# Sleeping set-up threads, a later request for output weights and later parameter transposes in a four-stage transformer kernel

## The chip, the cores and the metric

One core of one Trainium2 chip runs the whole program. The metric is the device time of one execution in microseconds (us). The built program fixes for each engine the order of its instructions; the engines are TensorE (PE; its weight loads are PEld), VectorE (DVE), ScalarE (ACT), GpSimd (POOL) and SyncE (SP, which here issues DMAs).

## The reference

Two blocks work on 512 tokens of width 1024, in float32. The lines that bear on the change, cut down:

```
# layer A: differential attention
q, k = rms_norm(h @ w_q), rms_norm(h @ w_k)          # 8 heads x 2 x 64
lam  = exp(sum(lam_q1*lam_k1)) - exp(sum(lam_q2*lam_k2)) + lam_init
bias = rel_table[t5_bucket(pos_q - pos_k)]           # positions are an input
a    = softmax(where(causal, q @ k.T / 8 + bias, -1e30))
o    = (a[:, 0] - lam * a[:, 1]) @ v                 # then rms_norm per head
h    = h + o @ a_w_o
# conv-gated FFN, twice (l = 0, 1): width-3 causal convolution with ffn_conv_w[l], ffn_conv_b[l]
h    = h + (silu(g) * a) @ ffn_w_out[l];  h = h + (p[l] @ w_proj) * sigmoid(rms_norm(h) @ w_gate)
# layer B: latent attention; its low-rank projection w_dkv is 1024 x 320
# second block: sparse attention (bias rows from rel_bias), convolution, gated linear
# attention, then a gated FFN, a per-layer embedding and a last norm
```

## The kernel before, in words

**Arithmetic.** A float32 matrix product is made of three products in the format fp32r: each operand is split in a high and a low part, and `mm3` issues low weight x high data, high weight x high data, high weight x low data. A weight arrives by DMA in a raw buffer `wr` (two buffers, issued by SP); ACT writes its high part `wh`, DVE the low part `wl = gain*wr - wh`. The data's parts are the tiles `X_83` (high, written by ACT from a transposed PSUM tile) and `X_84` (low, DVE). In attention the same split gives `qs`, `kh` (ACT) and `qs`, `kl` (DVE), each from a PSUM tile `tr` of four transposed 128x128 blocks.

**PSUM.** Accumulators have four banks, transposes two (`tr`), and two more (`s`) serve scores and transposes. A bank is written again only when its last reader is done, so a `tr` group on the PE waits for the DVE and ACT copies of the group two before it.

**Order of the work.** The program is written as generator threads (class `Order`): a thread gives way by yielding a planned time, a flag or a free bank, and the loop resumes whichever is due by a planned clock. `sleep(ns)` yields a planned time that many nanoseconds ahead, `due()` the planned end of what is recorded, `wait(flags)` until others have set them, `bank("tr")` until a bank is planned free. A tile scheduler then puts every engine's instructions in their final order. Nearly all instructions carry the line of a helper: L148 (recording), L285 (`mm`), L295 (`tr`). DMAs of weights are L378, of parameter rows `colr` L360.

**Start of layer A** (`layer_a`, from L711). The four token tiles are normed (`xn = h*ss`), transposed and split into `X`. Around that stand the test whether positions are consecutive (`pos_test`: tiles `praw`, `p`, `fl`, `posfi`; its result is loaded by every engine at L607, and L610 branches over a block that ordinary positions don't need), minus lambda (tiles `lt`, `ls`, `nlam`; four broadcasts issued on POOL at L733) and the bias rows (`rel_rows`: one-hot `oh` times table `tb`, result `rv`, stored as `rowsA`). These are recorded in line, not in threads.

**Middle of layer A.** `produce` makes four pairs of heads' queries and keys and two halves of values in the order p0 v0 p1 p2 p3 v1, then the product with `a_w_o`, whose four first weight tiles are 128x1024. `fqk[3]` are the flags of the last pair's four token tiles. `lane` runs the attention of the pairs: `sb = s + xn` (bias), exponentials `wT`, then `o`, normed to `on` by `sub_norm`.

**Parameters** (`columns`, L649). Its last part, `third` (L683), transposes `ffn_conv_w`, `ffn_conv_b` of l = 0 and l = 1 (tiles `cw0`, `cw1`) and the second block's convolution parameters from raw rows `colr` to columns, one PE transpose and one DVE copy each.

**Start of layer B** (L1127). The four token tiles t0 to t3 are multiplied with the 320 columns of `w_dkv`: 24 matmuls each. Beside it stand the rope tables (`ang`, `rn`, `rr`, `sin`, `cos`, with gains `kr`, `qr`), the norms of what comes out (`cn`, `kx`, `ky`, `kz`) and the second block's bias rows (`rel_rows` again, stored as `rowsR`), recorded in line ahead of the tiles.

Of the kernel before, what the change touches and what calls it, by code (L numbers as in the profile page):

```python
# [184 lines left out]
class Model:  # L185
    def __init__(self, ctx, tc, I, O):
        self.tc, self.I, self.O = tc, I, O
        self.n, self.rings = 0, {"acc": [], "tr": [], "s": []}
        self.od, self.g = Order(), {}
        nc = self.nc = Issue(self.od, tc.nc)  # L190
        self.acc, self.wu, self.xs, self.cr, self.sl = Slots(4), Slots(WB), Slots(2), Slots(3), Slots(2)
        pool = lambda name, **k: ctx.enter_context(tc.tile_pool(name=name, **k))
        self.cp = pool("cp", bufs=1)
        self.hp = pool("hp", bufs=1)
        self.wp = pool("wp", bufs=4)
        self.st = pool("st", bufs=4)
# [152 lines left out]
    def rows_T(self, out, rows):  # L349
# [17 lines left out]
        self.cr.give()  # L367


    def weight(self, n, parts, gain=None):  # L370
# [165 lines left out]

    def rel_rows(self, pp, table, name):

        nc = self.nc
        tb = pp.tile([33, 8], F32, name=self.uid("tb"), tag="tb")  # L540
        nc.vector.memset(tb, NEG)
        nc.scalar.dma_start(tb[:32, :], table)
        oh = pp.tile([33, 640], F32, name=self.uid("oh"), tag="oh")
        nc.scalar.dma_start(oh, self.I["c_onehot"])
        rv = pp.tile([8, 640], F32, name=self.uid("rv"), tag="rv")
        for c0, n in ((0, 512), (512, 128)):
            ps = self.ptile("tr")
            self.mm(ps[:8, :n], tb, oh[:, c0:c0 + n], True, True)
            nc.vector.tensor_copy(rv[:, c0:c0 + n], ps[:8, :n])
        row = self.dp.tile([8, 640], F32, name=name, tag=name)  # L550
        nc.sync.dma_start(row, rv)
        return row

# [24 lines left out]

    def pos_test(self, la):

        nc = self.nc
        fi = la.tile([1, 1], I32, name="posfi", tag="posfi")
        with self.phase("pos0") as pp:
            T = lambda shape, dt, tag: pp.tile(shape, dt, name=self.uid(tag), tag=tag)
            raw = T([1, S], I32, "praw")
            nc.scalar.dma_start(raw, self.I["positions"])
            hf, lf = self.pos_parts(T, raw, [1, S])
            dh, dl = T([1, S - 1], F32, "p3"), T([1, S - 1], F32, "p4")
            nc.vector.tensor_sub(dh, hf[:, 1:], hf[:, :S - 1])
            nc.vector.tensor_sub(dl, lf[:, 1:], lf[:, :S - 1])  # L590
            nc.vector.scalar_tensor_tensor(dl, dh, 4096.0, dl, op0=ALU.mult, op1=ALU.add)
            nc.vector.tensor_scalar(dl, dl, 1.0, None, op0=ALU.not_equal)
            fl = T([1, 1], F32, "fl")
            nc.vector.tensor_reduce(fl, dl, axis=AX.X, op=ALU.max)
            nc.vector.tensor_copy(fi, fl)
        return fi

# [51 lines left out]
    def columns(self, first):  # L649
# [33 lines left out]
        def third():  # L683
# [4 lines left out]
            self.cw = []  # L688
            for l in range(2):
                w = cp.tile([P, 176], F32, name=f"cw{l}", tag=f"cw{l}")  # L690
                self.cw.append(w.rearrange("p (i m) -> p i m", i=4))
# [19 lines left out]
    def layer_a(self, nxt):  # L711
# [11 lines left out]
        with self.phase("la") as pp:  # L723
            T1 = lambda name: pp.tile([P, 1], F32, name=name, tag=name)

            B = [self.rel_tile(f"biasB{i}", [1 + NT, 2]) for i in range(4)]
            fi = self.pos_test(pp)
            self.columns(False)
            qg, kg, sg = self.g["a_q_norm"], self.g["a_k_norm"], self.g["a_sub_norm"]

            lt = pp.tile([P, 4, 64], F32, name="lt", tag="wT", bufs=WTS)
            for i, nm in enumerate(("a_lam_q1", "a_lam_k1", "a_lam_q2", "a_lam_k2")):
                nc.gpsimd.dma_start(lt[:, i, :], I[nm][0].partition_broadcast(P))  # L733
            ls = pp.tile([P, 2], F32, name="ls", tag="ls")
            nc.vector.tensor_mul(lt[:, 0, :], lt[:, 0, :], lt[:, 1, :])
            nc.vector.tensor_mul(lt[:, 2, :], lt[:, 2, :], lt[:, 3, :])
            nc.vector.tensor_reduce(ls[:, 0:1], lt[:, 0, :], axis=AX.X, op=ALU.add)
            nc.vector.tensor_reduce(ls[:, 1:2], lt[:, 2, :], axis=AX.X, op=ALU.add)
            nc.scalar.activation(ls, ls, AF.Exp)
            nlam = T1("nlam")  # L740
            nc.vector.tensor_sub(nlam, ls[:, 1:2], ls[:, 0:1])
            nc.vector.tensor_scalar(nlam, nlam, -LAM_INIT, None, op0=ALU.add)

            flags = lambda: [Flag() for _ in range(NT)]
# [59 lines left out]
            def produce():  # L804
                for job in A_ORDER.split():
                    yield from (pair if job[0] == "p" else values)(int(job[1]))
                made.done = True

                for c in range(2):
# [13 lines left out]
            def fetch():  # L823
                for i, t in [(i, t) for i in range(4) for t in range(NT)]:
                    n = (t + 1) * P
                    if t == 0 and i < 3:
                        self.rel_fill(B[i + 1][0], row[2 * i + 2:2 * i + 4])
                    yield from self.xs.take()
# [11 lines left out]
            def lane():  # L840
                while steps:
# [16 lines left out]
                    if ob[1] == 4:  # L858
                        od.add(self.sub_norm(pp, ob[0], t, half, sg, made, fo[half][t], qns, obs), 0)

            od.add(produce(), 1)
            with self.phase("rel") as pr:
                row = self.rel_rows(pr, I["rel_bias_table"], "rowsA")
                self.rel_fill(B[0][0], row[:2])
                od.run(begun)
                which.append(self.bias_a(B, fi))
            fB.done = True
# [67 lines left out]
    def ffn_ple(self, x, token_of, src, combine, W_out, gain, p, w_gate, w_proj, ple_gain, nxt, name):  # L935
# [4 lines left out]
        with self.phase(name) as pp:  # L940
# [186 lines left out]
    def layer_b(self, x, nxt):  # L1127
# [3 lines left out]
        with self.phase("lb") as pp:  # L1131
# [11 lines left out]
            with self.phase("lb0") as p0:  # L1143
                cos, sin = self.rope_tables(p0)
                row = self.rel_rows(p0, I["rel_bias_2"], "rowsR")
                gpe = self.bcast_row(p0, I["k_pe_norm"], 64, "gkpe")
# [57 lines left out]
                od.add(down(), 1)  # L1204
                od.run(ready)

                for f in fkv:
# [3 lines left out]
            with self.phase("lb1") as p1:  # L1211
# [4 lines left out]
                def produce():  # L1216
                    for ch in range(8):
# [4 lines left out]
                        if ch == 4:  # L1222
                            self.rel_fill(self.rows_c, row)
                        chunk[ch] = [None, None]
# [760 lines left out]
```

## Time and profile before

| | |
|---|---|
| median of 3 runs | 2270.88 us (2266.21 to 2273.49) |
| profiled execution | 2270.06 us, of which 2268.3 us from the first to the last instruction (the span) |
| PE busy | 2197.4 us, 97% of the span |
| DVE / ACT / POOL busy | 59% / 47% / 8% |
| mean granted PE clock | 0.988 of full speed |

All times of rows are microseconds from the start of the span. Some 71 us of the span have no matmul in them; where these lie and what ended each is read from the timeline of the PE, where a row's bracket gives the idle time before it and the instruction that ended it.

### The profile page before, as it was taken

The page shows a single profiled execution, that of the slowest core. Times are in us where ns is not written, and L with a number is a line of the kernel's source. Part 1 is how long each engine was busy: PE and PEld are TensorE (multiplying, and loading weights), DVE is VectorE, ACT ScalarE, POOL GpSimd, SP SyncE. Part 2 cuts the span into 40 slices and gives each one's busy share as a digit, 9 for nine tenths or more (in the row PEclk, how much of TensorE's full clock was granted, in tenths as well). Part 3 has the DMA queues.
Part 4 walks back from the last instruction along what each step waited for, and adds up shares of the span by engine and source line. Part 5 has one row for each costly group of instructions (what it writes and reads, how often), then busy time and mean ns, then how long its engine had stood idle before and what let it go on. Part 6 is the DMA issues. An engine that isn't in the chain of part 4 may idle for free.

```text
span 2268.3 us, 30282 instructions
## 1 busy us (share of the span) xinstructions
PE 2197.4 (97%) x11166; PEld 1861.9 (82%) x11166; DVE 1336.6 (59%) x2885; ACT 1062.0 (47%) x2102; POOL 173.0 (8%) x232
## 2 busy tenths in 40 slices
PE   7987999999999999999999999999999999999998
PEld 5866798888887888888988888889978888888886
DVE  6668656446545777767565366357977643333344
ACT  4547445334444565555454254254657543323333
POOL 3123000000001121210000000001010000000000
PEclk9999999999999999999999999999989999999999
DMA  6323123332332412212133233234430123323322
GB/s 190 99 63 93 59 84 98 103 98 84 107 98 80 128 43 59 68 40 82 54 107 102 94 103 97 79 98 122 99 91 22 54 66 101 99 91 99 99 89 82
DMA packets 168839, 200.01 MB, mean 88 GB/s; under 512 B 19201, under 2 KB 123709, under 8 KB 168688
## 3 DMA queue, kind: packets, MB, share of 16 engines
q1 hardware_dynamic: 165172, 194.77, 28.1%
q10 hardware_dynamic: 2940, 2.02, 0.3%
q0 software_dynamic: 576, 1.26, 0.3%
q8 instruction: 88, 1.44, 0.3%
q14 instruction: 63, 0.52, 0.1%
HBM read 195.87 MB, written 7.38 MB: 90 GB/s over the span
## 4 chain that ended last, share of the span: by engine, by line
PE 91%; DVE 4%; ACT 1%; DMA 1%; issue 1%; POOL 0%; DVEq 0%; POOLq 0%; SPq 0%; ACTq 0%
PE acc L285 82%; PE s L285 4%; PE tr L295 4%; PE tr L285 1%; DVE wl L148 1%; DVE sb L148 1%; PE s L295 0%; DVE ss L148 0%; DVE X L148 0%; ACT wh L148 0%; DMA xn<-biasB 0%; DVE qs L148 0%; ACT wT L148 0%; DVE qn L148 0%; DMA tb<-rel_bias 0%
## 5 line engine op out<-in xcount | busy, mean ns | idle before, releaser
L285 PE MATMUL acc<-X,wh 128*128 128x512 f32 (+1 forms) x2592 | 734.9, 370 | 4.0 <-DVE X L148 4.0
L285 PEld LDWEIGHTS acc<-X,wh 128*128 128x128 f32 x2592 | 469.9, 189 | 85.0 <-DVE X L148 4.7
L285 PE MATMUL acc<-wh,X 128*128 128x512 f32 (+4 forms) x1664 | 502.0, 380 | 0.2 <-DVE X L148 0.2
L285 PE MATMUL acc<-X,wl 128*128 128x512 f32 (+1 forms) x1296 | 474.7, 369 | 0.0
L148 ACT ACTIVATE wh<-wr,gcol 128x512 fp32r<-128x512 f32 (+5 forms) x480 | 289.6, 656 | 208.4 <-PE acc L285 123.8
L148 DVE SCALAR_TENSOR_TENSOR wl<-wr,gcol,wh 128x512 fp32r<-128x512 f32 (+5 forms) x480 | 306.1, 674 | 131.5 <-ACT wh L148 129.5
L285 PEld LDWEIGHTS acc<-wh,X 128*128 128x128 f32 x1664 | 309.9, 190 | 45.9 <-DVE X L148 0.7
L285 PE MATMUL acc<-wl,X 128*128 128x512 f32 (+4 forms) x832 | 322.4, 388 | 7.3 <-DVE qn L148 3.3
L285 PEld LDWEIGHTS acc<-X,wl 128*128 128x128 f32 x1296 | 244.2, 189 | 40.8
L148 DVE TENSOR_TENSOR wl<-wr,wh 128x1024 fp32r<-128x1024 f32 (+1 forms) x134 | 152.5, 1144 | 183.8 <-ACT wh L148 183.6
L148 POOL TENSOR_TENSOR ss<-ss,mhalf 128x1 f32<-128x1 f32 (+3 forms) x140 | 128.9, 923 | 1727.4 <-DVE ss L148 1703.0
L148 ACT ACTIVATE wh<-wr 128x1024 fp32r<-128x1024 f32 (+1 forms) x134 | 132.5, 995 | 238.9 <-PE acc L285 191.2
L285 PE MATMUL acc<-wh,hh 128*128 128x512 f32 x528 | 205.7, 390 | 0.0
L285 PE MATMUL acc<-wl,hh 128*128 128x512 f32 x528 | 204.5, 389 | 0.0
L285 PE MATMUL acc<-wh,hl 128*128 128x512 f32 x528 | 203.7, 390 | 0.0
L285 PEld LDWEIGHTS acc<-wl,X 128*128 128x128 f32 x832 | 158.1, 190 | 32.8 <-DVE qn L148 3.6
L148 DVE SCALAR_TENSOR_TENSOR cv<-acc,cw,cv 128x511 f32<-128x511 f32 (+1 forms) x176 | 126.1, 745 | 95.2 <-ACT cv L148 94.4
L148 DVE TENSOR_TENSOR h<-h,acc 128x512 f32<-128x512 f32 x120 | 81.6, 684 | 61.3 <-PE acc L285 60.8
L285 PEld LDWEIGHTS acc<-wl,hh 128*128 128x128 f32 x528 | 99.1, 188 | 20.5
L285 PEld LDWEIGHTS acc<-wh,hl 128*128 128x128 f32 x528 | 99.1, 188 | 20.4
L285 PEld LDWEIGHTS acc<-wh,hh 128*128 128x128 f32 x528 | 99.1, 188 | 20.4
L148 ACT ACTIVATE wT<-tr 128x128 f32<-128x128 f32 (+3 forms) x160 | 68.8, 435 | 91.4 <-PE tr L295 90.6
(312 smaller groups left out, 2688.5 us busy)
## 6 DMA issues: line engine op xcount, KB each, us to landing
wr<-ffn_w_in SPq DMA_DIRECT2D x160, 256.0 KB
wr<-ffn_w_out SPq DMA_DIRECT2D x40, 512.0 KB
wr<-ple_w_gate SPq DMA_DIRECT2D x24, 512.0 KB
wr<-ffn_w_gate SPq DMA_DIRECT2D x40, 256.0 KB
wr<-ffn_w_up SPq DMA_DIRECT2D x40, 256.0 KB
wr<-ffn_w_down SPq DMA_DIRECT2D x20, 512.0 KB
wr<-a_w_qkv SPq DMA_DIRECT2D x32, 256.0 KB
wr<-b_w_o SPq DMA_DIRECT2D x16, 512.0 KB
```

What stands on the lines that cost most here:

```text
L148: return fn(*args, **kw)
L285: self.nc.tensor.matmul(out, lhsT=a, rhs=b, start=start, stop=stop)
L295: self.nc.tensor.transpose(out, src, self.ident[:src.shape[0], :src.shape[0]])
```

## The change

1. At the start of layer A the positions' test, minus lambda and the bias rows become three threads (`pos_test`, `minus_lambda`, `rel`, each wrapped by the new `flagged`), started after `produce`. Each issues its DMAs, sleeps 8000, 12000 or 4000 planned ns and then does its work; `pos_test` also yields `due()` between its steps. Lambda's four broadcasts move from POOL's queue to ACT's. The program runs until the three flags are set before it goes on to `bias_a` with the branch.
2. `produce` waits for `fqk[3]` before it asks for the first weights of `a_w_o`.
3. `third` waits for the flag `fed` before the convolution parameters of l = 1; `fed` is set when the first FFN starts. So two transposes and copies of `cw1` and one of the second block's parameters move from layer A to that FFN; their DMAs keep their place on SP to within some rows.
4. In layer B `rel_rows` is a thread with a sleep of 4000 ns, and the wait for its flag stands after the first tiles' flag `ready`.

```
+    @staticmethod
+    def flagged(thread, flag):
+        yield from thread
+        flag.done = True
...
-    def rel_rows(self, pp, table, name):
+    def rel_rows(self, pp, table, name, out):
...
+        yield self.sleep(4000)
         for c0, n in ((0, 512), (512, 128)):
+            yield from self.bank("tr")
...
+    def pos_test(self, pp, fi):
+        raw = T([1, S], I32, "praw")
+        nc.scalar.dma_start(raw, self.I["positions"])
+        yield self.sleep(8000)
...
             for l in range(2):
+                if l:
+                    yield from self.wait(self.fed)
...
                 made.done = True
+                yield from self.wait(*fqk[3])
...
+            def minus_lambda():
+                lt = pp.tile([P, 4, 64], F32, name="lt", tag="wT", bufs=WTS)
+                for i, nm in enumerate(("a_lam_q1", "a_lam_k1", "a_lam_q2", "a_lam_k2")):
+                    nc.scalar.dma_start(lt[:, i, :], I[nm][0].partition_broadcast(P))
+                ls = pp.tile([P, 2], F32, name="ls", tag="ls")
+                yield self.sleep(12000)
...
             od.add(produce(), 1)
...
+                for f, thread in zip(early, (rel(), self.pos_test(pr, fi), minus_lambda())):
+                    od.add(self.flagged(thread, f), 0)
                 od.run(begun)
+                for f in early:
+                    od.run(f)
                 which.append(self.bias_a(B, fi))
...
             od.add(main(), 1)
+            self.fed.done = True
...
-                row = self.rel_rows(p0, I["rel_bias_2"], "rowsR")
+                row, frow = [], Flag()
+                od.add(self.flagged(self.rel_rows(p0, I["rel_bias_2"], "rowsR", row), frow), 0)
...
                 od.run(ready)
+                od.run(frow)
```

**Place 1, the start.** DVE of before, from the second tile's statistic on; `wl_104` is the second weight pair, `lt` the second product of lambda vectors (it needs the third and fourth broadcast):

```order
L148 TENSOR_SCALAR ss_120<-ss_120 128x1
L148 TENSOR_SCALAR p_186<-p_186 1x511
L148 SCALAR_TENSOR_TENSOR wl_104<-wr_102,gcol_86,wh_103 128x512
L148 TENSOR_REDUCE fl_191<-p_186 1x1
L148 SCALAR_TENSOR_TENSOR wl_104<-wr_102,gcol_86,wh_103 128x512
L148 TENSOR_SCALAR xn_119<-h,ss_120 128x1024
L148 TENSOR_TENSOR lt<-lt 128x64
L148 CAST posfi<-fl_191 1x1
L148 TENSOR_TENSOR X_84<-tr_125,X_83 128x4x128
L148 TENSOR_TENSOR X_84<-s_132,X_83 128x4x128
L148 TENSOR_REDUCE ls<-lt 128x1
```

DVE of the change, from the first normed tile `xn_113` (in before it stands behind the two `wl_94`) to the low halves of the first tile's `X_84`:

```order
L148 TENSOR_SCALAR xn_113<-h,ss_114 128x1024
L148 TENSOR_TENSOR p_272<-p_268 1x511
L148 TENSOR_TENSOR praw_273<-p_269 1x511
L148 SCALAR_TENSOR_TENSOR wl_94<-wr_92,gcol_86,wh_93 128x512
L148 TENSOR_TENSOR lt<-lt 128x64
L148 SCALAR_TENSOR_TENSOR wl_94<-wr_92,gcol_86,wh_93 128x512
L148 SCALAR_TENSOR_TENSOR praw_273<-p_272,praw_273 1x511
L148 TENSOR_SCALAR ss_120<-ss_120 128x1
L148 TENSOR_REDUCE ls<-lt 128x1
L148 TENSOR_TENSOR lt<-lt 128x64
L148 TENSOR_TENSOR X_84<-tr_125,X_83 128x4x128
L148 TENSOR_TENSOR X_84<-s_132,X_83 128x4x128
```

ACT of the change, from the first tile's square on:

```order
L148 ACTIVATE xn_113,ss_114<-h 128x1024
L863 DMA lt<-a_lam_q 128x64
L863 DMA lt<-a_lam_k 128x64
L863 DMA lt<-a_lam_q 128x64
L148 ACTIVATE wh_93<-wr_92,gcol_86 128x512 x2
L863 DMA lt<-a_lam_k 128x64
L148 ACTIVATE xn_119,ss_120<-h 128x1024
```

The second `lt` now stands ahead of the first tile's `X_84`, and its fourth broadcast is issued by ACT behind two halves of `wh_93`; the three others are issued ahead of those. DVE's load of `posfi` for the branch (L610, now L618) stands seven rows after the second half of `wl_104`, and half of the next weight's split, `wl_323`, has moved ahead of it.

**Place 2, the middle of layer A.** DVE of before; `tr_3783` and `tr_3810` are the last two groups of transposes of the last pair, `wl_4332` and `wl_4338` the third and fourth weight tile of `a_w_o` (the first two, `wl_3959` and `wl_3965`, stand six and two rows further up):

```order
L148 TENSOR_TENSOR wl_4332<-wr_4330,wh_4331 128x1024
L148 SCALAR_TENSOR_TENSOR qs_3423<-tr_3783,gcol_196,qs_3423 64x2x128
L148 TENSOR_REDUCE ss_4000<-on_3998 128x4
L148 TENSOR_SCALAR ss_4000<-ss_4000 128x4
L148 TENSOR_TENSOR wl_4338<-wr_4336,wh_4337 128x1024
L148 SCALAR_TENSOR_TENSOR qs_3423<-tr_3810,gcol_196,qs_3423 64x2x128
L148 TENSOR_REDUCE ss_4014<-on_4012 128x4
L148 TENSOR_TENSOR on_3998<-o_2556,ss_4000 128x512
L148 SCALAR_TENSOR_TENSOR kl_3425<-tr_3783,gcol_196,kh_3424 64x2x128
L148 SCALAR_TENSOR_TENSOR kl_3425<-tr_3810,gcol_196,kh_3424 64x2x128
L148 TENSOR_SCALAR ss_4014<-ss_4014 128x4
L148 SCALAR_TENSOR_TENSOR qs_3423<-tr_3783,gcol_196,qs_3423 64x2x128
```

DVE of the change, the same stretch; the last two groups are `tr_3747` and `tr_3774`, the weight tiles `wl_4318` and `wl_4324` (the first two stand ten and seven rows further up):

```order
L148 TENSOR_TENSOR wl_4318<-wr_4316,wh_4317 128x1024
L148 SCALAR_TENSOR_TENSOR kl_3410<-tr_3747,gcol_174,kh_3409 64x2x128
L148 TENSOR_TENSOR on_3965<-o_2552,ss_3967 128x512
L148 TENSOR_TENSOR wl_4324<-wr_4322,wh_4323 128x1024
L148 SCALAR_TENSOR_TENSOR qs_3408<-tr_3774,gcol_174,qs_3408 64x2x128
L148 TENSOR_REDUCE ss_3981<-on_3979 128x4
L148 SCALAR_TENSOR_TENSOR qs_3408<-tr_3747,gcol_174,qs_3408 64x2x128
L148 SCALAR_TENSOR_TENSOR kl_3410<-tr_3774,gcol_174,kh_3409 64x2x128
L148 TENSOR_SCALAR ss_3981<-ss_3981 128x4
L148 SCALAR_TENSOR_TENSOR kl_3410<-tr_3747,gcol_174,kh_3409 64x2x128
L148 SCALAR_TENSOR_TENSOR qs_3408<-tr_3774,gcol_174,qs_3408 64x2x128
L148 TENSOR_TENSOR on_3979<-o_2624,ss_3981 128x512
```

All four weight splits still stand ahead of the last keys' `kl`. From the first split to the last `kl` there are 22 rows in before and 27 in the change, where four rows of the first scores' `sb`, which stood behind that `kl`, now stand ahead of it.

**Place 3, the start of layer B.** PE of before, from the last matmuls of t0 and t1 on; `tr_7988` and `tr_7991` are the bias rows, `tr_8143` the high half of tile t2's transposes, `acc_8180` tile t2:

```order
L285 MATMUL acc_8100<-wh_8050,X_83 128x320
L285 MATMUL acc_8100<-wh_8050,X_84 128x320
L285 MATMUL tr_7988<-oh_7985,tb_7982 8x512
L285 MATMUL tr_7991<-oh_7985,tb_7982 8x128
L295 MATMUL tr_8143<-ident,xn_7900 128x128 x4
L285 MATMUL acc_8180<-wl_8027,X_83 128x320
```

PE of the change, from the eighteenth matmul on of those 24 of tile t2 (`acc_8162`); `tr_8084` and `tr_8166` are the bias rows, `tr_8148` and `s_8155` tile t3's transposes, `acc_8219` tile t3:

```order
L285 MATMUL acc_8162<-wl_8039,X_83 128x320
L285 MATMUL acc_8162<-wh_8038,X_83 128x320
L285 MATMUL acc_8162<-wh_8038,X_84 128x320
L285 MATMUL tr_8084<-oh_8010,tb_8007 8x512
L285 MATMUL acc_8162<-wl_8039,X_83 128x320
L285 MATMUL acc_8162<-wh_8038,X_83 128x320
L285 MATMUL acc_8162<-wh_8038,X_84 128x320
L295 MATMUL tr_8148<-ident,xn_8001 128x128 x4
L295 MATMUL s_8155<-ident,xn_8001 128x128 x4
L285 MATMUL tr_8166<-oh_8010,tb_8007 8x128
L285 MATMUL acc_8219<-wl_8015,X_83 128x320
L285 MATMUL acc_8219<-wh_8014,X_83 128x320
```

DVE of the change, from tile t3's norm `xn_8001` on:

```order
L148 TENSOR_SCALAR xn_8001<-h,ss_8002 128x1024
L148 TENSOR_SCALAR ss_8201<-ss_8201 128x1
L148 TENSOR_SCALAR qr_7991<-qr_7991 128x4x32
L148 SCALAR_TENSOR_TENSOR cn_8094<-acc_8045,ss_8087,gckv_7997 128x256
L148 TENSOR_SCALAR kx_8096<-acc_8045,ss_8087 128x64
L148 TENSOR_TENSOR kr_7980<-cos_7972,gkpe_7978 128x4x32 x2
L148 TENSOR_TENSOR qr_7990<-cos_7972,gqpe_7987 128x4x32 x2
L148 SCALAR_TENSOR_TENSOR cn_8137<-acc_8105,ss_8130,gckv_7997 128x256
L148 TENSOR_SCALAR kx_8139<-acc_8105,ss_8130 128x64
L148 TENSOR_SCALAR ss_8201<-ss_8201 128x2
L148 TENSOR_TENSOR ky_8097<-kx_8096,kr_7981 128x32 x2
L148 TENSOR_TENSOR kz_8098<-kx_8096,kr_7980 128x64
```

The bias rows have moved behind t2's matmuls on the PE. On DVE the norm of t3 has moved behind the sine gains `kr`, `qr`; the low half `X_84` of t3 follows one row after this piece.

## Rows read from the trace of the kernel before

**Rows 1.** Page, section 1: busy time, share of the span, instructions.

```profile
PE 2197.4 (97%) x11166; PEld 1861.9 (82%) x11166; DVE 1336.6 (59%) x2885; ACT 1062.0 (47%) x2102; POOL 173.0 (8%) x232
```

**Rows 2.** Timeline of DVE, start: start us, us, what, [idle before <- what ended it].

```profile
9.84 0.23 DVE L148 TENSOR_TENSOR lt<-lt 128x64 f32<-128x64 f32 x1 [2.86 <-DMA lt<-a_lam_k]
...
9.98 1.27 DVE L148 TENSOR_TENSOR p<-p 1x511 f32<-1x511 f32 x2
...
13.23 0.73 DVE L148 TENSOR_SCALAR xn<-h,ss 128x1024 f32<-128x1024 f32 x1
```

**Rows 3.** Timeline of ACT, start.

```profile
0.81 0.53 ACTq L586 DMA_DIRECT2D praw<-positions  x1
...
9.67 1.33 ACT L148 ACTIVATE wh<-wr,gcol 128x512 fp32r<-128x512 f32 x2 [3.87 <-DMA wr<-a_w_qkv]
```

**Rows 4.** Instructions of tile praw: duration ns min/median/max, first and last start us.

```profile
L572 DVE TENSOR_SCALAR p<-praw x1: 414/414/414, 2.3 to 2.3; 1x512 int32<-1x512 int32 x1
```

**Rows 5.** DMAs of tile lt, issued on POOL.

```profile
DMA to landing us min/median/max: 6.1/7.6/7.9
```

**Rows 6.** Timeline of the PE, start.

```profile
14.02 1.12 PE L295 MATMUL tr<-ident,xn 128*128 128x128 f32 x4 [8.80 <-DVE ss L148]
```

**Rows 7.** Timeline of DVE, middle of layer A.

```profile
201.62 1.21 DVE L148 TENSOR_TENSOR wl<-wr,wh 128x1024 fp32r<-128x1024 f32 x1
...
207.82 1.23 DVE L148 TENSOR_TENSOR wl<-wr,wh 128x1024 fp32r<-128x1024 f32 x1 [1.37 <-ACT wh L148]
...
216.76 0.90 DVE L148 SCALAR_TENSOR_TENSOR kl<-tr,gcol,kh 64x256 fp32r<-64x256 f32 x2
...
217.88 0.69 DVE L148 CUSTOM_DVE_ANT_0 sb<-s,xn 128x512 f32<-128x512 f32 x1 [0.23 <-PE tr L295]
```

**Rows 8.** Timeline of the PE, middle of layer A.

```profile
217.40 0.85 PE L295 MATMUL tr<-ident,sb 128*128 128x128 f32 x2 [8.48 <-DVE kl L148]
```

**Rows 9.** Windows: length, busy us (instructions) PE, PEld, DVE, ACT, POOL; granted clock; DMA share.

```profile
120.00:200.00 80.00, 68.02 (x336) 54.70 (x335) 59.44 (x170) 48.47 (x118) 24.30 (x28) 0.96 0.28 81
215.00:220.00 5.00, 2.60 (x9) 2.16 (x10) 4.32 (x11) 3.09 (x9) 2.27 (x3) 0.50 0.02 6
220.00:225.00 5.00, 4.70 (x28) 4.03 (x27) 4.74 (x18) 3.67 (x13) 0.00 (x0) 0.81 0.02 1
738.00:744.00 6.00, 5.31 (x20) 5.01 (x20) 5.67 (x25) 2.81 (x5) 0.00 (x0) 0.50 0.64 201
744.00:747.00 3.00, 2.69 (x19) 2.19 (x17) 1.29 (x7) 1.92 (x7) 0.00 (x0) 0.98 1.00 265
```

**Rows 10.** Instructions of tile colr on the PE: ns min/median/max.

```profile
L295 PE MATMUL tr<-ident,colr x8: 219/241/280, 5.0 to 136.4; 88*128 88x88 f32 x4, 16*128 16x16 f32 x1, 3*128 3x3 f32 x1, 66*128 66x66 f32 x1
```

**Rows 11.** Copies into tile cw on DVE: ns min/median/max.

```profile
L148 DVE COPY cw<-tr x4: 236/246/250, 112.9 to 129.8; 128x88 f32<-128x88 f32 x4
```

**Rows 12.** Timeline of the PE, start of layer B.

```profile
735.31 1.23 PE L285 MATMUL tr<-oh,tb 33*8 33x512 f32 x4 [2.90 <-DMA tb<-rel_bias]
737.09 0.98 PE L295 MATMUL tr<-ident,xn 128*128 128x128 f32 x4 [0.55 <-DVE rv L148]
738.76 0.63 PE L285 MATMUL acc<-wl,X 128*128 128x320 f32 x1 [0.69 <-ACT X L148]
...
746.30 0.41 PE L285 MATMUL acc<-wl,X 128*128 128x320 f32 x1 [0.17 <-ACT X L148]
...
750.36 0.27 PE L295 MATMUL tr<-ident,ky 128*128 128x128 f32 x1
```

**Rows 13.** Timeline of ACT, issue of the table's DMA in layer B.

```profile
730.85 0.33 ACTq L542 DMA_DIRECT2D tb<-rel_bias  x1
```

**Rows 14.** Timeline of DVE, start of layer B, tile t3's norm and after.

```profile
739.81 0.75 DVE L148 TENSOR_SCALAR xn<-h,ss 128x1024 f32<-128x1024 f32 x1
740.47 0.48 DVE L148 TENSOR_TENSOR kr<-sin,gkpe 128x128 f32<-128x128 f32 x2
...
743.66 0.49 DVE L148 TENSOR_TENSOR ky<-kx,kr 128x32 f32<-128x32 f32 x4
```

More of the change, by code (lines that the diff above doesn't have):

```diff
@@ L188, in __init__ @@
         self.n, self.rings = 0, {"acc": [], "tr": [], "s": []}
-        self.od, self.g = Order(), {}
+        self.od, self.g, self.fed = Order(), {}, Flag()
         nc = self.nc = Issue(self.od, tc.nc)
@@ L551, in rel_rows @@
         nc.sync.dma_start(row, rv)
-        return row
+        out.append(row)
     def rel_fill(self, m, row):
@@ L577, in pos_parts @@
         return hf, lf
-    def pos_test(self, la):
+    def pos_test(self, pp, fi):
         nc = self.nc
[L582 to L596, printed above, removed]
+        T = lambda shape, dt, tag: pp.tile(shape, dt, name=self.uid(tag), tag=tag)
+        raw = T([1, S], I32, "praw")
+        nc.scalar.dma_start(raw, self.I["positions"])
+        yield self.sleep(8000)
+        hf, lf = self.pos_parts(T, raw, [1, S])
+        dh, dl = T([1, S - 1], F32, "p0"), T([1, S - 1], F32, "praw")
+        yield self.due()
+        nc.vector.tensor_sub(dh, hf[:, 1:], hf[:, :S - 1])
+        nc.vector.tensor_sub(dl, lf[:, 1:], lf[:, :S - 1])
+        yield self.due()
+        nc.vector.scalar_tensor_tensor(dl, dh, 4096.0, dl, op0=ALU.mult, op1=ALU.add)
+        nc.vector.tensor_scalar(dl, dl, 1.0, None, op0=ALU.not_equal)
+        yield self.due()
+        fl = T([1, 1], F32, "fl")
+        nc.vector.tensor_reduce(fl, dl, axis=AX.X, op=ALU.max)
+        nc.vector.tensor_copy(fi, fl)
     def bias_a(self, B, fi):
@@ L726, in layer_a @@
             B = [self.rel_tile(f"biasB{i}", [1 + NT, 2]) for i in range(4)]
-            fi = self.pos_test(pp)
+            fi = pp.tile([1, 1], I32, name="posfi", tag="posfi")
             self.columns(False)
             qg, kg, sg = self.g["a_q_norm"], self.g["a_k_norm"], self.g["a_sub_norm"]
[L731 to L742, printed above, removed]
             flags = lambda: [Flag() for _ in range(NT)]
@@ L826, in fetch @@
                     if t == 0 and i < 3:
-                        self.rel_fill(B[i + 1][0], row[2 * i + 2:2 * i + 4])
+                        self.rel_fill(B[i + 1][0], row[0][2 * i + 2:2 * i + 4])
                     yield from self.xs.take()
@@ L859, in lane, with rel @@
                         od.add(self.sub_norm(pp, ob[0], t, half, sg, made, fo[half][t], qns, obs), 0)
+            nlam = T1("nlam")
+            def minus_lambda():
[4 more added lines that the diff above has]
+                yield self.sleep(12000)
+                nc.vector.tensor_mul(lt[:, 0, :], lt[:, 0, :], lt[:, 1, :])
+                nc.vector.tensor_mul(lt[:, 2, :], lt[:, 2, :], lt[:, 3, :])
+                nc.vector.tensor_reduce(ls[:, 0:1], lt[:, 0, :], axis=AX.X, op=ALU.add)
+                nc.vector.tensor_reduce(ls[:, 1:2], lt[:, 2, :], axis=AX.X, op=ALU.add)
+                nc.scalar.activation(ls, ls, AF.Exp)
+                nc.vector.tensor_sub(nlam, ls[:, 1:2], ls[:, 0:1])
+                nc.vector.tensor_scalar(nlam, nlam, -LAM_INIT, None, op0=ALU.add)
             od.add(produce(), 1)
             with self.phase("rel") as pr:
-                row = self.rel_rows(pr, I["rel_bias_table"], "rowsA")
-                self.rel_fill(B[0][0], row[:2])
+                row, early = [], [Flag() for _ in range(3)]
+                def rel():
+                    yield from self.rel_rows(pr, I["rel_bias_table"], "rowsA", row)
+                    self.rel_fill(B[0][0], row[0][:2])
+                for f, thread in zip(early, (rel(), self.pos_test(pr, fi), minus_lambda())):
+                    od.add(self.flagged(thread, f), 0)
                 od.run(begun)
+                for f in early:
+                    od.run(f)
                 which.append(self.bias_a(B, fi))
@@ L1222, in produce @@
                         if ch == 4:
-                            self.rel_fill(self.rows_c, row)
+                            self.rel_fill(self.rows_c, row[0])
                         chunk[ch] = [None, None]
```

## The prediction, made before the changed kernel ran

> **What bounds the kernel now.** I read the page first: the PE is busy 2197.4 us [rows 1], so of the span of 2268.3 us only some 71 us hold no matmul. This change adds and removes no product of the GEMMs, so all it can give back lies in those gaps and in stretches that run at the lower clock. I then went through the timeline of the PE for gaps, and for each looked at the engine named in its bracket. Three lie beside edited code. At the start the PE waits 8.80 us for the first normed tile [rows 6]. In the middle of layer A it waits 8.48 us, because the `tr` bank that it wants next is held until DVE has made the last keys' `kl` [rows 8]: from 217.40 - 8.48 = 208.9 on; afterwards the granted clock is 0.50 for five microseconds and 0.81 for five more [rows 9]. At the start of layer B it waits 2.90 us for the bias table's DMA, then 0.55 and 0.69 us [rows 12], and from 738 to 744 the clock is at 0.50, the lower level of 1.2 GHz [rows 9]. A gap counts for the end here, since after each of these the PE goes on with little idle time up to the last stage; what is saved on DVE or ACT alone counts for nothing.
>
> **Edit 1, the start.** What it adds on the issuing side is cheap. The one-hot and table DMAs now precede `praw` on ACT, but ACT has nothing else at 0.81 [rows 3]. Three of lambda's broadcasts go out before ACT's first high parts of weights at 9.67, for which it has stood idle 3.87 us [rows 3]: hidden. If that cover were gone each would cost about the 0.53 us of an issue [rows 3].
>
> What it moves is on DVE. Before, DVE is idle 2.86 us up to 9.84, when lambda's first product finds its data [rows 2]. In the change the first `xn` (0.73 us) and the two position differences (1.27 us) stand ahead of that point, as the order shows; together 2.00 us of work [rows 2] that fills idle time. Against that, the first weight split comes next and has to wait for ACT's first half, 9.67 + 1.33/2 = 10.3 [rows 3], so the chain restarts 0.5 us later than at 9.84. Net 2.0 - 0.5 = 1.5 us less. The PE has its first tile transposed long before 14.02 [rows 6], but without the split it can't multiply.
>
> What it adds is a wait. The second `lt` now stands ahead of the first tile's `X_84`, and its last broadcast is issued by ACT behind both halves of `wh_93`, at 9.67 + 1.33 = 11.0 [rows 3]. DVE gets there at about 12.8: from 10.3, what it did before between 9.84 and 13.23 less the two differences, 3.4 - 1.3 = 2.1 us [rows 2], and some 0.3 us for a statistic and a second reduction (estimates between the rows' 0.23 and 0.73). With a landing time L the wait is L - 1.8 us if positive, and behind it stand `X_84`, the next splits and `xn`, all of which the PE needs, and on ACT the exponential of `ls`. Before holds no broadcast on ACT's queue, so L is bounded by neighbours: `praw`, one row, was issued at 0.81 and used at 2.3, 1.5 us [rows 3, 4]; the table in layer B, on the same queue, was issued at 730.85 and used at 735.31, 4.5 us [rows 12, 13]; the same four broadcasts from POOL landed in 6.1 to 7.9 us [rows 5]. I take 3 us, halfway between the two rows of ACT's queue. The term is -1.5 + 1.2 = **-0.3 us**; the bounds are -1.5 (L at or under 1.8) and -1.5 + 6.1 = +4.6 (L = 7.9).
>
> The Trainium skill, "DMA: Bandwidth & Descriptors", section "Anatomy of one DMA — SWDGE (gpsimd) path", gives about 2.0 us fixed per DMA; no row here lands lambda's broadcasts that quickly, and by that figure this term would be an estimated -1.3 and the whole sum 1 us lower.
>
> **Edit 3, the parameters.** Three PE transposes of 219 to 280 ns [rows 10] and three copies of about 0.25 us [rows 11] leave layer A and are paid again in the first FFN. From 120 to 200 the PE is busy 68.0 of 80 us [rows 9]: it waits there now and then, mostly for DVE, so leaving may save something; in the FFN the transposes are paid in full and the copies hide, since DVE is busy 59% of the span [rows 1]. Gain at most 0.75 (all of DVE's), loss at most 0.75 (all of the PE's, if layer A hid them): **-0.4 us**, because DVE is what is waited for where they stood.
>
> **Edit 2, the wait of `a_w_o`.** If it took the four 128x1024 splits out of DVE's way, the 8.48 us would go, and with it the low clock: 2.60 x 0.5 + 4.70 x 0.19 = 2.2 us [rows 9], 10.7 in all. The built order speaks against that. All four splits still stand among the last pair's `qs` and `kl`, ahead of the last `kl`. So the stall stays, and I compare its length. From the first split, at 201.62, to the end of the last `kl`, 216.76 + 0.90 = 217.66, the 22 rows of before took 16.0 us, 1.37 of them waiting for a weight's high part [rows 7]. In the change there are 27 rows. Four are the first two scores' pieces, 2 x 0.69 = 1.4 us that before paid after the stall [rows 7]; the fifth is one more small statistic or `qs`, about 0.5. With all waits kept, the last `kl` comes 1.9 us later for 1.4 us of work done early, a loss of 0.5; without the 1.37 us of waiting, since the first two weight tiles stand three to four rows further ahead of the others, a gain of 0.9. On the PE the wait is then cut in three, one for each of the last banks, instead of one; its sum stays near 8.5. I take **-1.0 us**, nearer the gain; bounds -10.7 and, with the three waits keeping the clock down for another five microseconds at 0.50, +0.5 + 2.5 = +3.
>
> **Edit 4, layer B.** Of the present wait 2.90 + 0.55 + 0.69 = 4.1 us [rows 12] goes, since t2's matmuls now precede the bias rows. Those 24 take (750.36 - 746.30)/24 = 0.17 us each at nearly full clock [rows 12], 4.1 us in all. The gap before 735.31 began at 732.4; with 0.4 for four transposes moved ahead, t2 is done at about 736.9, and the table has landed by then. What is late next is tile t3: its norm ends at 739.81 + 0.75 = 740.56 now [rows 14]. In the change the rope chain runs while before it waited for the bias row (some 1.9 us earlier), but the norm stands behind the sine gains (0.96 [rows 14] and two small rows, 1.4); `X_84` and one copy leave, 0.96. So 740.56 - 1.9 + 1.4 - 0.96 = 739.1, and the PE waits 2.2 us. Then t3's low half stands behind eleven rows like those from 740.47 to 744.15, 3.7 us [rows 14] less the sine gains' 0.96 plus 0.5 for `kz` and statistics: 739.1 + 3.2 + 0.7 = 743.0, while the PE has transposes and two matmuls up to 740.6, so it waits another 2.4 us. From 743.0 the remaining 22 matmuls take 3.7 us at full clock, end 746.7, against 750.36: -3.7. At the lower clock, which the rows show from 738 to 744 behind the waits of before [rows 9], they take about twice that: end 750.4, no gain. The clock had returned by 744 in before, so part of the stretch is fast: **-2.0 us**, about halfway; bounds -3.7 and 0.
>
> **The rest.** The order of layer A between 25 and 330 is dealt anew by moved times. I put nothing on that and plus or minus 3 us in the range, a quarter of the 12 us in which the PE is idle from 120 to 200 [rows 9].
>
> Sum: -0.3 - 0.4 - 1.0 - 2.0 = -3.7 us. The profiled execution took 2270.06 us (span 2268.3 and 1.8 around it), 0.8 us under the median of 2270.88, so it is typical: 2266.4 on its scale, **2267.2 us** on that of the median.
>
> **The rivals.**
> *A, the middle stall goes.* If the two first splits, further ahead, free DVE in time, the stall and the low clock shrink by most of 10.7 us: 2270.9 - 0.3 - 0.4 - 10.7 - 2.0 = 2257.5. For it: DVE idles 1.37 us there for weights [rows 7]. Against it: the order. Half of it gives 2263.
> *B, a stall of the ring at another place.* Where a weight split lands ahead of the last reader of a `tr` bank, the PE stops as it does at 208.9. One more such place in layer A costs 8.48 + 2.2 us: 2267.2 + 10.7 = 2277.9, slower than before. It decides from a wait of about 4 us on (3.7 to be made up). For it: the whole layer is reordered and its transposes have two banks; against it: DVE's order shows no new pile of splits.
> *C, the fourth broadcast is late.* DVE and ACT then stand at the second `lt`: with POOL's 7.9 us [rows 5] the start term is +4.6 and the sum +1.2, 2272.1; it turns the gain to a loss from L = 6.7. Here the Trainium skill bears on the case: in "DMA: Bandwidth & Descriptors", section "Issuing engines are not separate DMA queues", it says that DMAs of all issuing engines run on the same sixteen engines, so the move would save issue time only; the rows of ACT's queue at 1.5 and 4.5 us lean against POOL's landing times [rows 3, 4, 12, 13].
> *D, layer B gives nothing,* because t3 waits behind rope work at the lower clock: 2269.2.
>
> **How the numbers follow.** The measurement can tell about 0.3%, 6.8 us, from no change, so faster means under 2264.1 and slower over 2277.7. The forecast with its own 2262 to 2271 has 0.48, A whole or half 0.22, B 0.13, C 0.10, D 0.07. Faster: A's 0.22, and a third of the forecast's (start at its lower bound, layer B at -3.7, a good reshuffle: -1.5 - 0.4 - 1.0 - 3.7 - 1 = -7.6), 0.38 in all. Slower: B and a tail of C, 0.14. Same: 0.48. The range runs from A, 2257, to the edge of B, 2277.
>
> **What would show it.** Right: DVE's second `lt` idle by about 1 us on a DMA from ACT; the PE in the middle still short of 8 to 10 us, ended by `kl`, with the four splits before it; in layer B no wait on the table but two of about 2 us, on `xn` and `X`. Wrong: the middle without a wait over 3 us; a wait over 4 us at the start on lambda; a new wait over 4 us on a `tr` reader between 30 and 330 us.

## The result, and the profile after

The changed kernel takes 2282.39 us (median of 5, 2279.13 to 2286.32) against 2270.88 us: ratio 1.0054 with a 95% interval of 1.0036 to 1.0073, some 12 us slower, and outside the range that was forecast. The page of its profiled execution (2280.97 us), section 1:

```profile
PE 2207.1 (97%) x11166; PEld 1869.3 (82%) x11166; DVE 1336.7 (59%) x2885; ACT 1060.8 (47%) x2102; POOL 168.3 (7%) x228
```

The idle time of the PE has hardly changed: 2279.3 - 2207.1 = 72.2 us, against 2268.3 - 2197.4 = 70.9 [rows 1]. It is the busy time that grew, by 9.7 us, and the mean granted clock fell from 0.988 to 0.985, which over the span is 7 us. So most of the loss is work that ran at the low level of the clock, and in layer A above all. The windows from 20 to 330 us, before and then changed (columns as in [rows 9]; the clock is the third number from the end):

```profile
20.00:330.00 310.00, 281.83 (x1495) 235.16 (x1494) 213.30 (x529) 162.74 (x357) 61.24 (x68) 0.96 0.30 89
```

```profile
20.00:330.00 310.00, 275.71 (x1394) 227.48 (x1393) 204.35 (x511) 155.14 (x345) 61.19 (x67) 0.94 0.29 87
```

The timeline of the PE in the changed kernel, its waits beside the edited code and its longest ones in layer A (those of 1.0 to 2.2 us between 20 and 170, of which before has more, are left out):

```profile
14.56 0.80 PE L285 MATMUL acc<-wh,X 128*128 128x512 f32 x1 [2.74 <-DVE X L148]
...
180.26 0.44 PE L295 MATMUL tr<-ident,sb 128*128 128x128 f32 x2 [2.99 <-ACT wT L148]
...
181.87 0.80 PE L285 MATMUL acc<-wl,X 128*128 128x512 f32 x1 [1.17 <-DVE qn L148]
...
214.45 0.63 PE L295 MATMUL tr<-ident,qn 128*128 128x128 f32 x4 [1.59 <-DVE kl L148]
...
221.55 0.45 PE L295 MATMUL tr<-ident,sb 128*128 128x128 f32 x1 [6.48 <-DVE kl L148]
...
222.79 0.47 PE L295 MATMUL tr<-ident,sb 128*128 128x128 f32 x1 [0.79 <-ACT wT L148]
...
270.68 0.79 PE L285 MATMUL s<-kh,qs 128*128 128x512 f32 x1 [3.75 <-DVE nm L148]
...
297.37 0.66 PE L295 MATMUL s<-ident,xn 128*128 128x128 f32 x4 [2.29 <-DVE xn L148]
...
300.67 1.09 PE L295 MATMUL tr<-ident,on 128*128 128x128 f32 x4 [2.64 <-DVE on L148]
...
752.44 0.63 PE L295 MATMUL tr<-ident,xn 128*128 128x128 f32 x4 [1.96 <-DVE ss L148]
...
755.53 0.69 PE L295 MATMUL tr<-ident,cn 128*128 128x128 f32 x2 [1.21 <-DVE X L148]
```

Windows of the changed kernel:

```profile
180.00:183.00 3.00, 1.57 (x5) 1.15 (x6) 2.93 (x8) 2.91 (x8) 1.39 (x2) 0.66 0.51 152
183.00:186.00 3.00, 3.00 (x10) 2.43 (x9) 1.11 (x3) 0.47 (x1) 0.40 (x1) 0.50 0.56 177
186.00:189.00 3.00, 3.00 (x12) 2.39 (x11) 0.43 (x2) 0.60 (x2) 0.00 (x0) 0.70 0.07 23
220.00:225.00 5.00, 2.50 (x7) 1.76 (x8) 4.39 (x12) 3.27 (x9) 2.29 (x4) 0.50 0.27 99
295.00:300.00 5.00, 0.74 (x5) 0.42 (x4) 3.69 (x8) 2.62 (x6) 1.56 (x2) 1.00 0.00 0
300.00:305.00 5.00, 4.33 (x16) 3.62 (x17) 1.97 (x3) 1.28 (x2) 0.00 (x0) 0.66 0.34 108
756.00:759.00 3.00, 3.00 (x14) 3.00 (x13) 3.00 (x14) 1.79 (x4) 0.00 (x0) 0.50 0.23 20
```

To see where the time goes I added up the PE's matmuls in their order, each at its cost at full clock, and read when both traces reach the same amount; this is good to 1 or 2 us. How far the changed kernel is behind, by the time in before:

| at (us of before) | 44.8 | 90.6 | 161.5 | 181.9 | 218.2 | 255.5 | 287.5 | 293.6 | 345.4 | 794.7 |
|---|---|---|---|---|---|---|---|---|---|---|
| behind by (us) | 0.0 | +0.2 | +0.5 | +4.4 | +6.5 | +8.1 | +5.5 | +12.9 | +13.0 | +11.4 |

So the start is even, layer A loses 13 us, above all at 175 to 190 us and in its last 10 us, the first FFN with the three moved transposes loses nothing, and layer B gives 1.6 us back. The wait of 3.75 us near 270, 1.64 us in before, leaves nothing behind: from 255.5 to 287.5 the lag falls.

### The profile page after: what moved, and what is told of

The parts are those of the page before. It is cut to its first block, busy times and chain, and to the rows that moved or that the text cites. A ratio compares the mean times of both kernels' runs of the same rounds, so it can differ in the third digit from the quotient of the medians.

```text
span 2279.3 us, 30291 instructions
## 1 busy us (share of the span) xinstructions
PE 2207.1 (97%) x11166; PEld 1869.3 (82%) x11166; DVE 1336.7 (59%) x2885; ACT 1060.8 (47%) x2102; POOL 168.3 (7%) x228
## 4 chain that ended last, share of the span: by engine, by line
PE 91%; DVE 4%; DMA 2%; ACT 1%; issue 1%; POOL 0%; DVEq 0%; POOLq 0%; SPq 0%; ACTq 0%
PE acc L285 81%; PE s L285 5%; PE tr L295 4%; PE tr L285 1%; DMA xn<-biasB 1%; DVE wl L148 1%; DVE sb L148 1%; PE s L295 0%; DVE ss L148 0%; ACT wh L148 0%; DVE X L148 0%; DVE qs L148 0%; POOL ss L148 0%; DMA biasB<-rowsA 0%; DVE qn L148 0%
## 5 line engine op out<-in xcount | busy, mean ns | idle before, releaser
L285 PE MATMUL acc<-wh,X 128*128 128x512 f32 (+4 forms) x1664 | 507.1, 384 | 2.7 <-DVE X L148 2.7
L148 ACT ACTIVATE cv<-acc,cw 128x512 f32<-128x512 f32 x88 | 65.9, 775 | 97.5 <-PE acc L285 97.5
```

What stands on the lines that cost most here:

```text
L148: return fn(*args, **kw)
L285: self.nc.tensor.matmul(out, lhsT=a, rhs=b, start=start, stop=stop)
```

## Experiments

Each is timed against the kernel before on the same chip, and two experiments are compared by these ratios; one per cent is 22.7 us.

**One edit at a time.** e1 is edit 1 alone, e2 edit 3 alone, e3 edit 4 alone, and e4 all but edit 3. Edit 2 needed no run: with it alone, every row of the PE and of DVE in the built order is that of before, and without it every row is that of the changed kernel.

```
# e4: the changed kernel
             for l in range(2):
-                if l:
-                    yield from self.wait(self.fed)
# e1: e4's edit, and in layer B the rows in line again, without sleep or flag
-                od.add(self.flagged(self.rel_rows(p0, I["rel_bias_2"], "rowsR", row), frow), 0)
+                for _ in self.rel_rows(p0, I["rel_bias_2"], "rowsR", row, True):
+                    pass
# e2: the kernel before
+                if l:
+                    yield from self.wait(self.fed)
...
+            self.fed.done = True
# e3: the kernel before
+                od.add(self.flagged(self.rel_rows(p0, I["rel_bias_2"], "rowsR", row), frow), 0)
...
                 od.run(ready)
+                od.run(frow)
```

> The kernel before with edit 1 alone (the three threads at the start of layer A; the other three edits are left out). Theory S, the start's threads re-deal the order of layer A badly: +10 to +13 us over before, with the long waits near 180, 270 and 300 us as in the changed kernel. Theory F, the later transposes re-deal it: 0 +- 2 us here, with the waits of before after 120 us. Theory L, any new deal of this layer's order lands somewhere by luck: a value of its own between -5 and +13, and other places of waits than in either kernel.

> The kernel before with edit 3 alone (the l = 1 parameters wait for the first FFN). Theory S: 0 +- 2 us. Theory F: +10 to +13 us. Theory L: a value of its own, and the three edits' effects do not add up to the changed kernel's +11.5.

> The kernel before with edit 4 alone (the bias rows of layer B as a thread). All theories: layer A as before, and -1 to -2.5 us from layer B, as the lag between the two traces falls from 13.0 to 11.3 us there. If it is 0 or a loss, that fall had another cause.

> The changed kernel without edit 3 (the l = 1 parameters are transposed in layer A as before). Theory S: +9 to +12 us over before. Theory F: -2 +- 2 us. Theory L: a value of its own, not e1 plus e3 unless its order in layer A is that of e1.

| | ratio to before | 95% interval |
|---|---|---|
| e1, edit 1 | 0.9993 | 0.9983 to 1.0002 |
| e2, edit 3 | 1.0052 | 1.0038 to 1.0065 |
| e3, edit 4 | 1.0000 | 0.9991 to 1.0009 |
| e4, edits 1, 2, 4 | 0.9984 | 0.9974 to 0.9993 |

The whole loss comes with edit 3, as theory F had it, and theory S falls. The rest of the change gives 0.16%, 3.6 us. Edit 4 can't be told from nothing by its time, but every trace shows it: from the first load of `w_dkv` to layer B's first score takes 87.2 to 88.6 us, mean 87.8, in the eight profiled kernels with edit 4, and 88.8 to 90.6, mean 89.6, in the eight without, so 1.8 us. And the PE runs layer A in one order in e1 and e4 (their rows part first at 726 us, in layer B), so the step from e1 to e4, 0.09% or 2.0 us, is edit 4's too, though no larger than its noise.

**Is it the absence of the transposes, or the new deal of the order?** e5 and e6 only change the first sleep of the parameters' thread; e7 does so with edit 3; e8 holds back the last transpose alone.

```
e5 (58000), e6 (64000): the kernel before; e7 (62000): e2
-            yield self.sleep(60000)
+            yield self.sleep(62000)
e8: the kernel before
+            yield from self.wait(self.fed)
             yield from self.rows_T(out, rows)          # the second block's parameters, gcol3
```

> The kernel before, with only the first sleep of the parameters' thread at 58000 planned ns in place of 60000: all transposes stay in layer A, and no work is added or left out. Theory L, any shift of planned times re-deals the order of layer A and the time falls by luck: somewhere between -5 and +13 us, with other waits than before near 180, 270 and 300 us. Theory M, it is the absence of the three transposes that opens those waits: within +-3 us of before, with none of the waits of 2 us and more at 180 and at 297 to 300 us.

> As e5 with 64000 planned ns. Theory L: another value than e5, in the same span. Theory M: within +-3 us of before.

> The kernel before with edit 3, and the first sleep at 62000 planned ns. Its order differs from that of e2 in a part of layer A only. Theory L: a value of its own, not that of e2 (+12). Theory M: +10 to +13 us, as e2.

> The kernel before with only the last of the three transposes (the second block's parameters) waiting for the first FFN; those of l = 1 stay in layer A. Theory L: a value of its own between -5 and +13 us. Theory M: a part of the loss, +2 to +6 us, by one of three transposes.

| | ratio to before | 95% interval |
|---|---|---|
| e5, 58000 | 0.9992 | 0.9983 to 1.0001 |
| e6, 64000 | 0.9965 | 0.9952 to 0.9979 |
| e7, edit 3 and 62000 | 1.0002 | 0.9993 to 1.0011 |
| e8, gcol3 alone later | 0.9976 | 0.9966 to 0.9986 |

Two planned microseconds on one sleep take the 12 us away (e7 against e2), and four give 8 us in a kernel that moves nothing out of layer A (e6). Theory M falls: it is the deal of layer A's order. e6 lies outside the span that I gave theory L, -5 to +13 us, so a deal can also win more than I had allowed for.

**What the bad deal does at the end of layer A.** The last three products of attention weights with v are, in before and in every kernel that isn't slower, those of tile 2 (6 matmuls), tile 3 and tile 3 (8 each). In the changed kernel and e2, and in no other so far, tile 2's comes last. The timeline of the PE in before, then in the changed kernel:

```profile
275.37 0.83 PE L285 MATMUL tr<-v,wT 128*128 128x128 f32 x6
...
278.49 1.16 PE L285 MATMUL tr<-v,wT 128*128 128x128 f32 x8 [1.85 <-ACT wT L148]
...
283.78 1.06 PE L285 MATMUL tr<-v,wT 128*128 128x128 f32 x8
...
294.25 0.60 PE L295 MATMUL tr<-ident,on 128*128 128x128 f32 x4
```

```profile
284.21 1.16 PE L285 MATMUL tr<-v,wT 128*128 128x128 f32 x8 [0.51 <-ACT wT L148]
...
287.60 1.05 PE L285 MATMUL tr<-v,wT 128*128 128x128 f32 x8
...
293.59 0.83 PE L285 MATMUL tr<-v,wT 128*128 128x128 f32 x6
...
294.48 0.60 PE L295 MATMUL tr<-ident,on 128*128 128x128 f32 x4
```

Its product is done at 294 instead of 276. The output product takes the tiles in order, so tile 3, whose `on` was transposed at 294.48, waits for tile 2's, which follows at 300.67; from 295 to 300 the PE is busy 0.74 us. In before tile 2's norm is long done by then, and matmuls of `a_w_o` fill the time until tile 3's `on` at 294.25. e9 puts this right in e2, e10 in the changed kernel, by one rule (`av2` counts tile 2's products of heads 6 and 7):

```
         v = vs[h // 4]
+        while qt == 3 and h >= 6 and self.av2 < 2:
+            yield lambda: self.av2 >= 2
         yield from wts.take()
...
+        self.av2 += qt == 2 and h >= 6
```

> e2 (edit 3 alone, +12 us) and in it one rule for the last attention pieces: the product with v of token tile 3 in the last two heads is not recorded before those of token tile 2. No work is added or left out; the order differs from e2's only from the last tenth of layer A on. Theory T, two thirds of the loss is the tail of layer A, where in e2 and the changed kernel tile 2's last product comes behind both of tile 3 and the output product, which takes the tiles in order, waits for it with nothing to cover it: the waits of 2.29 and 2.64 us near 297 and 300 us go, and the time falls by 7 to 9 us against e2, to +3 to +5 over before. Theory U, the tail only shows what was late anyway: -2 us or less against e2, and the waits turn up at another place.

> The changed kernel with the rule of e9. Theory T: 7 to 9 us less than the changed kernel, +2 to +5 us over before. Theory U: within 2 us of the changed kernel.

e9 is at 1.0029 (1.0020 to 1.0039), e10 at 1.0026 (1.0017 to 1.0035). Against the changed kernel's 1.0054 e10 gains 0.28%, 6.4 us, and its trace shows them where they were looked for: it is 6.5 us behind before at 255.5 and 6.1 at 293.6, where the changed kernel went to 12.9. The waits of 2.29 and 2.64 us are gone; the PE's timeline of e10 near the end of layer A:

```profile
282.11 0.63 PE L296 MATMUL tr<-ident,on 128*128 128x128 f32 x4 [1.47 <-DVE on L148]
...
283.52 0.50 PE L286 MATMUL acc<-wl,X 128*128 128x512 f32 x1 [0.45 <-ACT X L148]
...
293.30 1.16 PE L286 MATMUL tr<-v,wT 128*128 128x128 f32 x8 [1.12 <-ACT wT L148]
```

So theory T holds for its place, with a size of 5 to 6 us in place of 7 to 9 (e9 gains 0.23%, 5.2 us, against e2; both gains are clear of their noise, but not by much). Of what remains, some 6 us, its trace has 3 to 4 by 200 us and over 5 by 218.

> The changed kernel, all four edits, with the first sleep of the parameters' thread at 62000 planned ns as in e7. Theory L, the loss is the luck of one deal: e7's order in the middle (0 against before) with what edits 1 and 4 gave in e4 (-3.6): -1 to -5 us against before. If edit 3 costs by itself: +5 us or more.

> The changed kernel without edit 3 and with 64000 planned ns, as in e6 (-8 us with the start and layer B of before). If the parts add up: -8 - 3.6 = -10 to -12 us against before, faster than both kernels. If every deal is its own draw: anywhere from -12 to +5.

e11 is at 1.0000 (0.9991 to 1.0009): the loss is gone with all four edits in, though e4's 0.16% isn't added. e12 is at 0.9964 (0.9952 to 0.9976), 8 us faster than before and 20 us faster than the changed kernel; against e6 the gains of edits 1 and 4 are not added either. It beats both kernels. That these gains are lost is not shown, as such a difference is known to 3 or 4 us only. What is shown is which part of the edits matters: kernels with the same parameters' thread lie within 4 us of each other, whatever start and layer B they have (before 0, e1 -1.6, e4 -3.6; e2 and the changed kernel both +12; e7 +0.5, e11 0.0; e6 and e12 both -8), while this thread's timing alone spreads them over 20 us.

**The place at 180 us.** ACT's timeline in the changed kernel:

```profile
177.63 1.33 ACT L148 ACTIVATE wh<-wr,gcol 128x512 fp32r<-128x512 f32 x2 [1.56 <-DMA wr<-a_w_qkv]
...
179.64 0.57 ACT L148 ACTIVATE wT<-tr 128x512 f32<-128x512 f32 x1
```

The PE's wait of 2.99 us at 180.26 ends with `wT` at 179.64. This copy was queued behind two high parts of a weight, which waited 1.56 us for their DMA, and two exponentials. After it the clock is at 0.66, 0.50 and 0.70 up to 189. e13 lets DVE make this one copy, e14 adds the rule of e10.

```
-        nc.scalar.activation(wT[:, :qt + 1, :], pt, AF.Copy)
+        if (h, qt) == (3, 3):
+            nc.vector.tensor_copy(wT[:, :qt + 1, :], pt)
+        else:
+            nc.scalar.activation(wT[:, :qt + 1, :], pt, AF.Copy)
```

> The changed kernel with one copy moved: the transposed weights wT of head 3, tile 3 are copied by DVE in place of ACT (same values). In the changed kernel this copy stands on ACT behind two high parts of a weight that wait 1.56 us for their DMA, and the PE waits 2.99 us for it at 180 us and then runs at a clock of 0.50 to 0.66; on DVE it stands ahead of that weight's low part. The tail is that of the changed kernel. Theory Q, what is left of the loss after the tail is this place: no wait over 1.5 us near 180, and -4 to -7 us against the changed kernel, +5 to +8 over before. Theory N, the place is a symptom and the time is lost at the next wait: within 2 us of the changed kernel.

> e10 and e13 together: tile 2's last product first, and the copy on DVE. Theory Q: the two places are the loss, and the time is that of before or up to 3 us less (what edits 1 and 4 gave in e4): -4 to +2 us. Theory N: as e10, +4 to +8 us over before.

e13 is at 1.0047 (1.0035 to 1.0059), e14 at 1.0020 (1.0011 to 1.0028): 0.06 to 0.07% less than the changed kernel and e10, some 1.5 us, within their intervals. Theory Q's times don't come. (From e13 to e14, on one chip, the rule of e10 gains 0.27%, 6.1 us, for the third time.) The waits near 180 of e13, from the PE's timeline:

```profile
181.54 0.71 PE L285 MATMUL tr<-v,wT 128*128 128x128 f32 x4 [1.54 <-ACT wT L148]
...
183.26 1.16 PE L285 MATMUL tr<-v,wT 128*128 128x128 f32 x8 [0.67 <-DVE o L148]
...
185.84 0.80 PE L285 MATMUL acc<-wl,X 128*128 128x512 f32 x1 [1.43 <-DVE qn L148]
```

The wait of 2.99 us has split into two of 1.5 at the next places. In e14 it has hardly shrunk; the PE, then ACT:

```profile
178.90 0.71 PE L286 MATMUL tr<-v,wT 128*128 128x128 f32 x4 [2.69 <-ACT wT L148]
```

```profile
176.11 1.33 ACT L148 ACTIVATE wh<-wr,gcol 128x512 fp32r<-128x512 f32 x2 [1.58 <-DMA wr<-a_w_qkv]
...
178.48 0.36 ACT L148 ACTIVATE wT<-tr 128x256 f32<-128x256 f32 x1
```

In both the PE now waits for the next copy `wT`, which is still ACT's and stands behind the same kind of weight. So these two runs show that moving this one copy gains next to nothing. They don't clear the queue of ACT, and whether the loss near 180 would go with it is not shown. e13 keeps the tail of the changed kernel and its loss there, e14 does not.

## Why the prediction was wrong

**The step that failed is "The rest".** There I put nothing, and 3 us either way, on the new order of layer A between 25 and 330 us. It holds all of the loss: 13 us in the changed kernel's trace. The experiments with this order dealt anew but no rule or moved copy (e1, e2, e4 to e8, e11, e12) lie between -8 and +12 us: the bound should have been some 10 us, not a quarter of the PE's idle time, since a deal also decides how much of the work runs at the low clock and whether the stage's end is covered. And I costed **edit 3** by what it moves, three transposes and copies, -0.4 us. That price may stand, as the FFN shows no loss, but a thread that no longer takes its turn at the `tr` banks re-deals what comes after. None of the three signs of being wrong came, no wait over 4 us at a new place among them, and those of being right all did in kind: they watched the edited places, and the loss came in several shorter waits elsewhere and in the clock behind them.

**Rival B** came nearest, with 2277.9 and a chance of 0.13. I spoke against it with DVE's order. The place at 180 was in ACT's, where the row behind a weight that waits for its DMA was a reader of a bank; that it stood there is seen, that it costs the time there is not shown. The larger part was no stall of the ring but a tile in the wrong order at the stage's end. That order could be read from the built order of the PE ahead of the run.

**Edit 1** was forecast at -0.3 us with a wait of 1.2 us on lambda's fourth broadcast. e1 is 1.6 us faster, not to be told from nothing (interval -3.9 to +0.5). The wait came, 1.36 us, but out of two errors that cancel. DVE and ACT, start of the changed kernel:

```profile
13.68 0.23 DVE L148 TENSOR_TENSOR lt<-lt 128x64 f32<-128x64 f32 x1 [1.36 <-DMA lt<-a_lam_k]
```

```profile
6.74 0.72 ACT L148 ACTIVATE wh<-wr,gcol 128x512 fp32r<-128x512 f32 x1 [0.75 <-DMA wr<-a_w_qkv]
6.80 0.34 ACTq L863 DMA_DIRECT2D lt<-a_lam_k  x1
```

The first weights were split at 6.74, not at 9.67 [rows 3], so the fourth broadcast went out at 6.80 instead of 11.0; and it was used 6.9 us after that, not 3. Neither is one trace's luck: the first split starts at 6.7 to 7.0 in the eight traces with edit 1 and at 8.4 to 9.9 in the eight without, and from that issue to the use it is 6.1 to 7.7 us in those eight. The 2.0 us that the prediction set beside its sum are met by none of them, nor by POOL's 6.1 to 7.9 [rows 5]. By the Trainium skill, "DMA: Bandwidth & Descriptors", section "Issuing engines are not separate DMA queues", DMAs of all issuing engines share the same DMA engines, and issuing from several saves issue time only. The trace agrees: 6.9 us from ACT's queue lie among the 6.1 to 7.9 us of POOL's [rows 5]. Rival C's landing time was nearly right, and its loss was not, for the earlier issue.

**Edit 2** does nothing, as read from the order, and A didn't come. From the first split of `a_w_o` to the end of the last `kl` took 207.94 to 224.36 us, 16.4 against 16.0 before [rows 7], of which 1.1 us are the scores' two pieces, done ahead; my sum gave 17.9 with all waits for weights and 16.5 without. The stall was cut in three, 1.59 + 6.48 + 0.79 = 8.9 us against 8.48 [rows 8]: it stayed, as forecast, and the gain of 1.0 did not come; the lag grows by some 2 us from 181.9 to 218.2. And the cut is not edit 2's: e2 has the waits of 1.59 and 6.48 us without it, e4, which has it, one of 8.62.

**Edit 4** was forecast at -2.0 us; the traces show 1.8. The wait on the table went, and the two that were named came, for the norm 1.96 us (2.2 forecast) and for the low half 1.21 (2.4). The low clock came too: 0.50 from 756 to 759. So rival D fell.

Without edit 3 the forecast sum, -3.3 us, meets e4's -3.6 (-5.9 to -1.6), in part by luck: -1.0 of it is for edit 2, which does nothing. Edit 4's share came; what e1 has besides can't be told from nothing.

**What stays open** are some 4 to 5 of the 12 us: e14, with the tail put right and one copy moved, is still 0.20% above before (0.11 to 0.28%). By the same adding-up its trace is 4.4 us behind at 200 us and 5.6 at 345. So most of it comes up near 180, where the PE waits 2.69 us and then, from 180 to 190, runs at a mean clock of 0.67, before's at 1.00. Which rows of the deal cause it, no run here tells.

## What to carry to other kernels

Where a planner sets the order, cost an edit by the new order, not by the instructions that it moves: compare the built order at the end of each stage, and ask whether the last pieces come in the sequence in which the next product takes them. Then time the same kernel at a few values of an idle constant: if these spread as far as the edit's effect, the edit hasn't been measured, only one deal of the order. Look for copies that free a PSUM bank behind anything that waits for a DMA, on ACT as well as on DVE.

## What the runs showed that I had not expected

The same built order gave traces that part by 3 us: layer A of e3 is on the PE and DVE row for row that of before, and its first convolution in the FFN behind it starts 3.0 us earlier (319.1 against 322.1). The granted clock goes with it. After the same wait in the same order, 1.85 us at 278.49 in before (shown above) and 1.86 us in e3, the windows of the next 5 us are, in before and then in e3 with its wait:

```profile
279.00:284.00 5.00, 5.00 (x28) 4.54 (x28) 2.71 (x6) 1.90 (x4) 1.01 (x1) 0.66 0.00 0
```

```profile
277.50:282.50 5.00, 5.00 (x39) 4.42 (x38) 3.46 (x8) 2.35 (x4) 1.01 (x1) 1.00 0.01 3
...
277.01 1.16 PE L285 MATMUL tr<-v,wT 128*128 128x128 f32 x8 [1.86 <-ACT wT L148]
```

One trace is at 0.66 there with 28 matmuls in the window, the other at 1.00 with 39. So a wait of this length does not by itself settle what the clock does next, and a single trace places a loss to within some 3 us only. And idle time alone does not tell a loss: with 1.3 us more idle in the whole span the PE needed 11 us more, some 7 of them by the lower mean clock.
